# Sixteen operand products of a pair in one row, and six low-rank products kept together

## The chip, the cores and the metric

The kernel runs on one core of one Trainium2 chip. The metric is the device time of one execution in microseconds (us); the time before is the median of three runs, 1564.96 us (1563.26 to 1566.88). The profile is one execution recorded by the hardware profiler. Its engines are PE (TensorE, matrix products), PEld (its weight loads), DVE (VectorE), ACT (ScalarE), POOL (GpSimd) and SP (SyncE, which issues the transfers).

## The reference

Two layers of a hybrid decoder run over 512 tokens of width 1024 in float32. Each layer has one wide input projection, an RWKV-7 branch (8 heads of 64, a generalized delta rule), a latent attention branch, two gates, an output projection and a gated feed-forward with a convolution. What matters here is the RWKV-7 branch:

```python
log_w = -jax.nn.softplus(-(decay_base + jnp.tanh(p_w) @ w_decay_up)) - 0.5
decay = jnp.exp(-jnp.exp(log_w.astype(jnp.float32)))
iclr = jax.nn.sigmoid(iclr_base + p_a @ w_iclr_up)
kk = heads((p_k * k_k).astype(jnp.float32))
kk = kk * lax.rsqrt(jnp.sum(kk * kk, axis=-1, keepdims=True) + 1e-12)
k = p_k * (1.0 + (iclr - 1.0) * k_a)
...
def step(state, inp):
    r_t, w_t, k_t, v_t, a_t, b_t = inp
    sa = jnp.einsum('bhij,bhj->bhi', state, a_t)
    state = (state * w_t[:, :, None, :]
             + sa[..., None] * b_t[:, :, None, :]
             + v_t[..., None] * k_t[:, :, None, :])
    y_t = jnp.einsum('bhij,bhj->bhi', state, r_t)
    return state, y_t
```

The kernel does not step through 512 tokens. It cuts them into 8 chunks of 64, builds for each head and chunk the 128 x 128 product of scaled operands (`BK` with `AR`), masks it, solves the triangular part for all chunks, and then passes the state from chunk to chunk.

## The kernel before

Large products are done in three passes (high times high, low times high, high times low part of the operands; lines 253 to 255, tile `acc`). Weights come in units of eight 128 x 128 blocks, 24 products each; ACT rounds a unit to its high part (`whi`, line 203) and DVE takes the difference (`wlo`, line 204).

In the first stage of a layer the heads are taken in four pairs. The generator `pair(p)` is one pair's work in pieces, and a loop runs pieces of neighbouring pairs with projection and gate products between them. In order, `pair(p)` forms k, r and v; then two low-rank products `pw` and `pq` of 64 rows each, three passes (lines 540 and 541); from `pw` a Tanh on ACT (`z`, line 545), on DVE an addition (547) and a running sum (`L`, 550), from which come the decays; from `pq` another Tanh (`tad`, 560). Then come sums and transpositions for the normed key (570 and 578), the operands `AR` and `BK`, the bonus sum (618, read by 619) and v transposed (624, read by the copies to `Z` at 627). The last pieces are the operand products (635): for each half of the eight chunks, four chunks times two heads of the pair, into two banks `pA`. DVE multiplies both by the mask into `AM` (638), PE transposes `BKb` into a bank `pB` (643), and ACT copies that (644). The loop lets a gate's 24 products run between the halves. The low-rank products of pair p + 1 come just ahead of the operand products of pair p.

All these small results live in banks of one PSUM pool, tag `m`, with five buffers; three more hold `acc`. A bank can be written again when its last reader is done.

After the pairs comes the solve. DVE and ACT copy the triangular blocks (687), DVE transposes them (688) and works through 30 steps of a substitution (692, 694), transposes the result (696), and PE takes it from there (780). Meanwhile PE forms the latents (`lat`, read by DVE at 718).

The order on each engine is not the order of the code: a planner places every instruction by priorities and its own guess of when operands are ready. Within a `manual_schedule` block the named engine's instructions keep the order of the code. On the chip each engine then runs its list in that order; an instruction that waits holds up all behind it.

Of the kernel before, what the change touches and what calls it, by code (L numbers as in the profile page):

```python
# [159 lines left out]
def build(ctx, tc, x, pos, wst, vecd, constd, out):  # L160
    nc = tc.nc
    V, A, G, PE = nc.vector, nc.scalar, nc.gpsimd, nc.tensor
# [118 lines left out]
    def split(pool, src, scale, tag, bufs=None):  # L281

        hi = pool.tile([128, 512], F32R, name="hi", tag=tag, bufs=bufs)
        lo = pool.tile([128, 512], F32R, name="lo", tag=tag, bufs=bufs)
        if scale is None:
            A.copy(hi, src)
            V.tensor_tensor(lo, src, hi.bitcast(F32), ALU.subtract)
        else:
            A.activation(hi, src, AF.Copy, scale=scale)  # L289
            V.scalar_tensor_tensor(lo, src, scale, hi.bitcast(F32), ALU.mult, ALU.subtract)  # L290
        return hi, lo
# [141 lines left out]
    def mixer(l, ops, nrm, wks):  # L433
        with ExitStack() as mx:
            wk = wks.enter_context(pool(name=f"wk{l}", bufs=1))
            AM = wk.tile([128, 8, 8, 128], F32, name="AM")
            AR = [wk.tile([128, 8, 128], F32, name=f"AR{p}") for p in range(4)]
# [13 lines left out]
            with pool(name=f"ta{l}", bufs=2) as ta, pool(name=f"pa{l}", bufs=2, space=PSUM) as pa, \  # L451
# [7 lines left out]
                def mtile():  # L459
                    return pa.tile([128, 512], F32, name="m", tag="m", bufs=5)  # L460
# [62 lines left out]
                wah = split(ta, wa, None, "wah", 2)  # L523
                lw = []
# [5 lines left out]
                def pair(p):  # L530
# [4 lines left out]
                    v = shifted(4 + 3 * p, "v")  # L535
                    yield
                    pw, pq = mtile(), mtile()
                    for i, (w, xx) in enumerate(((0, 0), (0, 1), (1, 0))):
                        sl = slice(128 * p, 128 * p + 128)
                        PE.matmul(pw, lw[w][0:64, sl], wah[xx][0:64, :], start=i == 0, stop=i == 2)  # L540
                        PE.matmul(pq, lw[w][64:128, sl], wah[xx][64:128, :], start=i == 0, stop=i == 2)

                    z = TL("z")
                    z3 = z.rearrange("p (c t) -> p c t", t=65)
# [51 lines left out]
                    BK = ta.tile([128, 8, 128], F32, name="BK", tag="BK", bufs=2)  # L596
# [31 lines left out]
                               pV[64 * e:64 * e + 64, :].rearrange("p (c n) -> p c n", c=4))  # L628
                    yield

                    for hf in range(2):
                        pA = [mtile(), mtile()]
                        for c in range(4):
                            for hh in range(2):
                                PE.matmul(pA[hh][:, c * 128:c * 128 + 128], BK[64 * hh:64 * hh + 64, 4 * hf + c, :],  # L635
                                          AR[p][64 * hh:64 * hh + 64, 4 * hf + c, :], start=True, stop=True)
                        for hh in range(2):
                            V.tensor_tensor(AM[:, 2 * p + hh, 4 * hf:4 * hf + 4, :].rearrange("p (c e) n -> p c (e n)", e=2),
                                            pA[hh].rearrange("p (c n) -> p c n", c=2),
                                            maskA[:, None, :].to_broadcast([128, 2, 256]), ALU.mult)  # L640
                        pB = mtile()
                        for c in range(4):
                            PE.transpose(pB[:, c * 128:c * 128 + 128], BKb[:, 4 * hf + c, :], ident)  # L643
                        A.copy(BT[p][:, 4 * hf:4 * hf + 4, :].rearrange("p c n -> p (c n)"), pB)
                        yield

                pairs = [pair(p) for p in range(4)]
                for _ in range(3):
                    next(pairs[0])
# [30 lines left out]
            with pool(name=f"ti{l}", bufs=2) as ti, tc.manual_schedule(engines={PE.engine}):  # L680
# [95 lines left out]
                for b in range(2):  # L776
                    ps = sc()
                    for u in range(16 * b, 16 * b + 16):
                        for r0, c0 in half:
                            PE.matmul(ps[r0 + 32:r0 + 64, 32 * (u % 16):32 * (u % 16) + 32],  # L780
                                      AMu[r0:r0 + 32, u, c0 + 32:c0 + 64], T11[r0:r0 + 32, u, :],
                                      start=True, stop=True, tile_position=(r0, r0 + 32))
# [28 lines left out]
                for c in range(8):  # L811
                    i, e = divmod(c, 2)
# [17 lines left out]
                    for hd in (0, 4, 1, 5, 2, 6, 3, 7):  # L830
# [4 lines left out]
                                  start=True, stop=True, tile_position=(ur, ur))  # L835
# [173 lines left out]
    for l in range(DEPTH):  # L1009
# [7 lines left out]
        with pool(name=f"h{l + 1}", bufs=8, side="right") as hp, accs(f"accC{l}", 6):  # L1017
# [31 lines left out]
            with pool(name=f"ff{l}", bufs=44) as fp:  # L1049
# [11 lines left out]
                for i in range(FT):  # L1061
# [4 lines left out]
                    c = fp.tile([128, 528], F32, name="c", tag="ft", bufs=7)  # L1066
# [22 lines left out]
                if last:  # L1089
                    m = KT - 1  # L1090
                    ws = [W.get() for _ in range(FT)]
                    with tc.manual_schedule(engines={PE.engine}):
                        for f in range(2):
                            c = slice(256 * f, 256 * f + 256)
# [57 lines left out]
```

## Time and profile before

| | |
|---|---|
| median of the runs | 1564.96 us |
| the profiled execution, time | 1565.82 us |
| its span | 1564.0 us |
| mean granted clock of PE | 0.994 |
| PE busy | 1532.7 us, 98% |
| DVE busy | 913.5 us, 58% |
| ACT busy | 669.2 us, 43% |
| operand products (L635) | 256 instructions, 8 blocks of 16 in each layer |
| their place in the span | 83.8 to 182.5 us (layer 0), up to 955 us (layer 1) |

A row of the order of time has the start in us, the duration, the engine, the line, the operation, output and inputs, and the count of merged instructions; in brackets is the idle time of the engine ahead of it and what ended that. A float32 product counts as two instructions, so eight products are x16. A row of stretches has the start and end, the length, the busy time of PE with its instructions, the granted clock as a part of full speed, the share of the transfer engines and GB/s.

### The profile page before, as it was taken

The page shows a single profiled execution, that of the slowest core. Times are in us where ns is not written, and L with a number is a line of the kernel's source. Part 1 is how long each engine was busy: PE and PEld are TensorE (multiplying, and loading weights), DVE is VectorE, ACT ScalarE, POOL GpSimd, SP SyncE. Part 2 cuts the span into 40 slices and gives each one's busy share as a digit, 9 for nine tenths or more (in the row PEclk, how much of TensorE's full clock was granted, in tenths as well). Part 3 has the DMA queues.
Part 4 walks back from the last instruction along what each step waited for, and adds up shares of the span by engine and source line. Part 5 has one row for each costly group of instructions (what it writes and reads, how often), then busy time and mean ns, then how long its engine had stood idle before and what let it go on. Part 6 is the DMA issues. An engine that isn't in the chain of part 4 may idle for free.

```text
span 1564.0 us, 22128 instructions
## 1 busy us (share of the span) xinstructions
PE 1532.7 (98%) x8860; PEld 1233.0 (79%) x8860; DVE 913.5 (58%) x1510; ACT 669.2 (43%) x1020; POOL 184.4 (12%) x157
## 2 busy tenths in 40 slices
PE   8999999999999999999999999998999999999998
PEld 6888886668888888888878888765788888888887
DVE  6579795766555555533346768867564555554332
ACT  6445444663443333322244544457444333333222
POOL 1011101300311110100001121013012111100000
PEclk9999999999999999999999999999999999999999
DMA  6324322324323222333342333222352232222322
GB/s 208 115 95 139 124 83 69 96 86 155 122 89 101 95 95 94 100 116 115 108 149 94 109 108 117 81 65 92 101 171 92 96 106 95 94 95 96 103 98 81
DMA packets 57270, 166.05 MB, mean 106 GB/s; under 512 B 6352, under 2 KB 8528, under 8 KB 57168
## 3 DMA queue, kind: packets, MB, share of 16 engines
q1 hardware_dynamic: 57024, 164.48, 31.9%
q8 instruction: 69, 1.13, 0.3%
q14 instruction: 33, 0.27, 0.1%
q10 hardware_dynamic: 144, 0.16, 0.0%
HBM read 147.32 MB, written 17.30 MB: 105 GB/s over the span
## 4 chain that ended last, share of the span: by engine, by line
PE 92%; DVE 5%; ACT 1%; issue 1%; POOL 0%; DMA 0%; DVEq 0%; POOLq 0%; SPq 0%; ACTq 0%
PE acc L253 27%; PE acc L254 27%; PE acc L255 27%; PE sc L973 2%; PE pt L984 1%; PE po L992 1%; PE m L635 1%; DVE wlo L204 1%; PE xy L834 1%; PE m L643 1%; PE xy L844 1%; PE acc L947 1%; PE m L540 0%; DVE X L694 0%; DVE tm L692 0%
## 5 line engine op out<-in xcount | busy, mean ns | idle before, releaser
L253 PE MATMUL acc<-hi,whi 128*128 128x512 f32 (+1 forms) x1918 | 755.0, 394 | 6.1 <-ACT hi L289 5.2
L255 PE MATMUL acc<-hi,wlo 128*128 128x512 f32 (+1 forms) x1918 | 747.4, 390 | 0.8 <-DVE wlo L204 0.8
L254 PE MATMUL acc<-lo,whi 128*128 128x512 f32 (+1 forms) x1918 | 746.8, 389 | 0.0
L203 ACT CAST whi<-raw 128x1024 fp32r<-128x1024 f32 (+2 forms) x249 | 253.4, 1019 | 535.8 <-PE acc L254 463.3
L253 PEld LDWEIGHTS acc<-hi,whi 128*128 128x128 f32 x1918 | 361.2, 188 | 81.4 <-ACT hi L289 5.2
L255 PEld LDWEIGHTS acc<-hi,wlo 128*128 128x128 f32 x1918 | 361.2, 188 | 75.4 <-DVE wlo L204 1.3
L254 PEld LDWEIGHTS acc<-lo,whi 128*128 128x128 f32 x1918 | 361.5, 188 | 71.1 <-DVE lo L290 0.5
L204 DVE TENSOR_TENSOR wlo<-raw,whi 128x1024 fp32r<-128x1024 f32 (+2 forms) x249 | 303.3, 1220 | 178.2 <-ACT whi L203 177.8
L1072 POOL TENSOR_TENSOR c<-c,rstd 128x512 f32<-128x512 f32 x44 | 57.9, 1317 | 403.6 <-ACT c L1071 403.6
L1065 DVE TENSOR_TENSOR u<-acc,rstd 128x512 f32<-128x512 f32 x44 | 30.4, 692 | 104.4 <-PE acc L255 104.3
L1074 DVE TENSOR_TENSOR c<-c,acc 128x512 f32<-128x512 f32 x44 | 30.2, 687 | 86.4 <-POOL c L1072 86.4
L1071 ACT ACTIVATE c<-c 128x512 f32<-128x512 f32 x44 | 27.8, 632 | 81.7 <-DVE c L1070 81.7
L312 POOL TENSOR_TENSOR nv<-nv,cst 128x4 f32<-128x4 f32 (+1 forms) x10 | 10.0, 996 | 335.4 <-DVE nv L311 335.4
L348 POOL TENSOR_TENSOR nacc<-nacc,nsq 128x512 f32<-128x512 f32 x14 | 25.1, 1790 | 193.0 <-ACT nsq L347 193.0
L973 PE MATMUL sc<-K,q 128*128 128x128 f32 (+3 forms) x128 | 45.4, 451 | 1.3 <-DVE mn L976 1.0
L466 DVE TENSOR_TENSOR cur<-acc,rstd 128x512 f32<-128x512 f32 x28 | 19.1, 689 | 45.1 <-PE acc L255 37.6
L981 ACT ACTIVATE P<-P,mn 128x128 f32<-128x128 f32 (+3 forms) x64 | 35.1, 559 | 5.1 <-DVE mn L980 4.8
L979 ACT ACTIVATE P<-P,mn 128x128 f32<-128x128 f32 (+3 forms) x64 | 35.5, 556 | 3.7 <-DVE mn L976 3.5
L1068 ACT ACTIVATE c<-u,vec 128x512 f32<-128x512 f32 x44 | 35.7, 811 | 2.8 <-DVE u L1064 2.8
L976 DVE CUSTOM_DVE_ANT_0 P<-sc,cst 128x128 f32<-128x128 f32 (+3 forms) x64 | 30.4, 482 | 8.1 <-PE sc L973 5.5
L1070 DVE SCALAR_TENSOR_TENSOR c<-u,vec,c 128x512 f32<-128x512 f32 x44 | 33.1, 752 | 1.5
L1069 DVE SCALAR_TENSOR_TENSOR c<-u,vec,c 128x512 f32<-128x512 f32 x44 | 32.8, 746 | 1.8 <-ACT c L1068 1.8
(243 smaller groups left out, 1318.5 us busy)
## 6 DMA issues: line engine op xcount, KB each, us to landing
raw<-in_w SPq DMA_DIRECT2D x238, 512.0 KB, 3.3
gate_d<-gg SPq DMA_DIRECT2D x32, 256.0 KB, 2.0
AM<-gate_d SPq DMA_DIRECT2D x16, 256.0 KB, 4.2
gb<-gate_d SPq DMA_DIRECT2D x16, 256.0 KB, 3.2
h<-in_x SPq DMA_DIRECT2D x8, 256.0 KB, 4.3
rgate_d<-gt SPq DMA_DIRECT2D x8, 256.0 KB, 2.5
bl_d<-rk SPq DMA_DIRECT2D x8, 256.0 KB, 4.2
bl<-bl_d SPq DMA_DIRECT2D x8, 256.0 KB, 2.6
```

Source lines behind the costliest of these rows:

```text
L203: A.copy(hi, r)
L204: V.tensor_tensor(lo, r, hi.bitcast(F32), ALU.subtract)
L253: PE.matmul(ps, w[0], xx[0], start=first, stop=False)
L254: PE.matmul(ps, w[0], xx[1], start=False, stop=False)
L255: PE.matmul(ps, w[1], xx[0], start=False, stop=last)
L973: PE.matmul(sp[:, 0:n], qs[hh][:, 128 * b:128 * b + 128], ks[hh][:, 0:n], start=True, stop=True)
L979: A.activation(P[:, 0:n], P[:, 0:n], AF.Exp, bias=mn[:, 0:1], scale=-1.0, accum_out=mn[:, 1:2])
L981: A.activation(P[:, 0:n], P[:, 0:n], AF.Copy, scale=mn[:, 2:3])
L1068: A.activation(cc, u[:, 2:514], AF.Identity, bias=vc(l, "conv_b", i), scale=vc(l, "conv_w", 2 * FT + i))
L1069: V.scalar_tensor_tensor(cc, u[:, 1:513], vc(l, "conv_w", FT + i), cc, ALU.mult, ALU.add)
L1070: V.scalar_tensor_tensor(cc, u[:, 0:512], vc(l, "conv_w", i), cc, ALU.mult, ALU.add)
L1072: G.tensor_tensor(cc, cc, rstd, ALU.mult)
```

## The change

```diff
@@ pair(p)
                     pw, pq = mtile(), mtile()
-                    for i, (w, xx) in enumerate(((0, 0), (0, 1), (1, 0))):
-                        sl = slice(128 * p, 128 * p + 128)
-                        PE.matmul(pw, lw[w][0:64, sl], wah[xx][0:64, :], start=i == 0, stop=i == 2)
-                        PE.matmul(pq, lw[w][64:128, sl], wah[xx][64:128, :], start=i == 0, stop=i == 2)
+                    with tc.manual_schedule(engines={PE.engine}):
+                        for i, (w, xx) in enumerate(((0, 0), (0, 1), (1, 0))):
+                            sl = slice(128 * p, 128 * p + 128)
+                            PE.matmul(pw, lw[w][0:64, sl], wah[xx][0:64, :], start=i == 0, stop=i == 2)
+                            PE.matmul(pq, lw[w][64:128, sl], wah[xx][64:128, :], start=i == 0, stop=i == 2)
...
+                    pAs = [[mtile(), mtile()] for _ in range(2)]
+                    with tc.manual_schedule(engines={PE.engine}):
+                        for c in range(8):
+                            for hh in range(2):
+                                PE.matmul(pAs[c // 4][hh][:, c % 4 * 128:c % 4 * 128 + 128], BK[64 * hh:64 * hh + 64, c, :],
+                                          AR[p][64 * hh:64 * hh + 64, c, :], start=True, stop=True)
                     for hf in range(2):
-                        pA = [mtile(), mtile()]
-                        for c in range(4):
-                            for hh in range(2):
-                                PE.matmul(pA[hh][:, c * 128:c * 128 + 128], BK[64 * hh:64 * hh + 64, 4 * hf + c, :],
-                                          AR[p][64 * hh:64 * hh + 64, 4 * hf + c, :], start=True, stop=True)
+                        pA = pAs[hf]
                         for hh in range(2):
```

The same products are computed from the same operands. All sixteen products of a pair now stand in one row and write four banks, which are taken together; masks, transposes and copies stay in the two halves. The six low-rank products of a pair can no longer have another product between them. In the changed program the lines of the pair are named one higher up to the products (540 and 541 are 541 and 542), and three higher behind them (638 is 641, 643 is 646, 687 is 690, 718 is 721); the products are 636.

**PE, the first pair of layer 0**, from the last low-rank products of pair 1 to the first gate product. `m` is a bank, `AR_203` and `BK` the operands, `BKb` what is transposed; in brackets the engines whose progress an instruction waits for. Before:

```order
L540 MATMUL m<-hi,lw_429 128x512
L541 MATMUL m<-hi,lw_429 128x512
L635 MATMUL m<-AR_203,BK 128x128 [waits DVE_49,PE_49]
L635 MATMUL m<-AR_203,BK 128x128 [waits PE_49,Activation_49]
L635 MATMUL m<-AR_203,BK 128x128 x6
L643 MATMUL m<-cst,BKb 128x128 [waits DVE_49,Pool_49]
L643 MATMUL m<-cst,BKb 128x128 x3
L253 MATMUL acc<-hi,whi 128x512
```

and now:

```order
L541 MATMUL m<-hi,lw_429 128x512
L542 MATMUL m<-hi,lw_429 128x512
L636 MATMUL m<-AR_203,BK 128x128 [waits DVE_49,PE_49]
L636 MATMUL m<-AR_203,BK 128x128 [waits PE_49,Activation_49]
L636 MATMUL m<-AR_203,BK 128x128 x6
L636 MATMUL m<-AR_203,BK 128x128 [waits DVE_49]
L636 MATMUL m<-AR_203,BK 128x128 [waits Activation_49]
L636 MATMUL m<-AR_203,BK 128x128 x6
L646 MATMUL m<-cst,BKb 128x128 [waits DVE_49,Pool_49]
L646 MATMUL m<-cst,BKb 128x128 x3
L253 MATMUL acc<-hi,whi 128x512
```

The second eight products moved up by 24 gate products, with their waits on DVE and ACT; the transposes of the first half now stand behind all sixteen. In pairs 1 and 2, and in layer 1, the same moved.

**DVE, the same place**: the rows from the gate's product to the masks, as they stand now.

```order
L478 TENSOR_TENSOR gg<-acc,rstd 128x512
L204 TENSOR_TENSOR wlo<-raw,whi 128x1024
L548 TENSOR_SCALAR z<-z 128x8x64
L551 SCALAR_TENSOR_TENSOR L<-d_222,z 128x520
L641 TENSOR_TENSOR AM<-m,cst 128x512 x2
L611 TENSOR_TENSOR AR_204<-r,z 128x4x2x64
L641 TENSOR_TENSOR AM<-m,cst 128x512 x2
```

Down to the first two masks and L611 these rows are those of before, one for one; the second two masks came some rows later and follow at once now.

**DVE, where the solve begins** in layer 0, behind the last pair's masks. Before:

```order
L478 TENSOR_TENSOR gg<-acc,rstd 128x512
L204 TENSOR_TENSOR wlo<-raw,whi 128x1024
L638 TENSOR_TENSOR AM<-m,cst 128x512 x2
L687 COPY DX<-AM 32x1024 x2
L688 STREAM_TRANSPOSE X<-DX 128x1024
L692 TENSOR_TENSOR tm<-X 128x30
L694 TENSOR_TENSOR X<-X,tm 128x30
L692 TENSOR_TENSOR tm<-X 128x58
L718 TENSOR_TENSOR lat_1828<-acc,rstd 128x512
```

and now:

```order
L641 TENSOR_TENSOR AM<-m,cst 128x512 x4
L478 TENSOR_TENSOR gg<-acc,rstd 128x512
L204 TENSOR_TENSOR wlo<-raw,whi 128x1024
L690 COPY DX<-AM 32x1024 x2
L721 TENSOR_TENSOR lat_1852<-acc,rstd 128x512
L691 STREAM_TRANSPOSE X<-DX 128x1024
L204 TENSOR_TENSOR wlo<-raw,whi 128x1024
L695 TENSOR_TENSOR tm<-X 128x30
```

The last masks moved ahead of the gate's product, and the first latent's product moved ahead of the transposition that opens the solve. It is the same in layer 1. On SP only transfers of the rotary tables and of pair 2's bonus changed places with their neighbours, in layer 0.

## The prediction

> **What bounds the kernel now.** I read the page's span and chain of waits first, then the list of who waited for whom, then the order of time on PE, DVE and ACT around one product block.
>
> ```profile
> span 1564.0 us, 22128 instructions
> ...
> PE 1532.7 (98%) x8860; PEld 1233.0 (79%) x8860; DVE 913.5 (58%) x1510; ACT 669.2 (43%) x1020; POOL 184.4 (12%) x157
> ...
> PE 92%; DVE 5%; ACT 1%; issue 1%; POOL 0%; DMA 0%; DVEq 0%; POOLq 0%; SPq 0%; ACTq 0%
> ```
>
> TensorE carries the chain. Whatever makes PE stand still or saves it an instruction slot is paid or earned in full; work on DVE and ACT counts only where PE is made to wait for it. So the question is which waits the new order puts in front of PE. This is one block of products, pair 0 of layer 0, in order of time on PE:
>
> ```profile
> 83.04 0.50 PE L540 MATMUL m<-hi,lw 64*128 64x512 f32 x1
> ...
> 83.84 1.06 PE L635 MATMUL m<-AR,BK 64*128 64x128 f32 x16
> 84.84 0.66 PE L643 MATMUL m<-cst,BKb 128*128 128x128 f32 x4
> 85.25 0.47 PE L253 MATMUL acc<-hi,whi 128*128 128x512 f32 x1
> ...
> 90.59 0.39 PE L255 MATMUL acc<-hi,wlo 128*128 128x512 f32 x1
> 90.91 1.16 PE L635 MATMUL m<-AR,BK 64*128 64x128 f32 x16
> 92.00 0.66 PE L643 MATMUL m<-cst,BKb 128*128 128x128 f32 x4
> 92.41 0.48 PE L253 MATMUL acc<-hi,whi 128*128 128x512 f32 x1
> 92.72 0.40 PE L254 MATMUL acc<-lo,whi 128*128 128x512 f32 x1
> ```
>
> PE never stops here: low-rank products of the next pair from 83.04, eight products in 1.00 us, four transposes in 0.41, then 24 gate products (85.25 to 90.59 are 23 steps, 0.23 each), then the other eight products and four transposes. The readers are far behind. On ACT and on DVE, the same stretch:
>
> ```profile
> 85.41 0.69 ACT L545 ACTIVATE z<-m,der 128x512 f32<-128x512 f32 x1
> ```
>
> ```profile
> 84.04 0.68 DVE L478 TENSOR_TENSOR gg<-acc,rstd 128x512 f32<-128x512 f32 x1
> 84.64 1.21 DVE L204 TENSOR_TENSOR wlo<-raw,whi 128x1024 fp32r<-128x1024 f32 x1
> 86.13 0.43 DVE L547 TENSOR_SCALAR z<-z 128x512 f32<-128x512 f32 x1 [0.28 <-ACT z L545]
> 86.66 1.24 DVE L550 TENSOR_TENSOR_SCAN L<-d,z 128x520 f32<-128x520 f32 x1
> 87.82 1.26 DVE L638 TENSOR_TENSOR AM<-m,cst 128x512 f32<-128x512 f32 x2
> ```
>
> The Tanh that reads `pw` ends at 86.10, 2.3 us behind the start of the products. The mask that reads the first product bank ends at about 88.50 (two take 1.26, one 0.68), 3.7 us after the products. Today this lag costs nothing, because the 5.4 us of gate products lie between the block and the next request for those banks.
>
> **The change part by part.** *Banks.* There are five `m` banks. At the block of pairs 0, 1 and 2 they hold: one free, `pV` (read by the copies to Z), the bonus sum (read by L619), `pw` (read by the Tanh L545), `pq` (read later still). Now the first half takes the free one and that of `pV`, the transposes that of the sum; the second half comes 24 products later and takes `pw`'s bank and the first product bank again. After the change four banks are wanted at once: the fourth is `pw`'s, so the second product of the second half waits for the Tanh; and the transposes behind the sixteen products then find only the bank of the first products, so they wait for the first mask. These are the two waits that stand in the order shown above; the built program's wait counts are those of this Tanh and this mask. PE works in order, so behind them stand the 24 gate products and everything else.
>
> *Price of a block.* Nothing ahead of the Tanh or the first mask moves on ACT or DVE, and none of it waits for the held instructions, so both end when they end now. How soon PE follows a release is in the solve's rows further down: a transposition ends at 222.73 + 2.18 = 224.91 and PE starts at 224.97, 0.06 later. So the transposes start at 88.56. Without waits they would start at 83.84 + 2 x 1.00 = 85.84. PE loses 2.72 us, in two gaps: about 85.0 to 86.16 and 87.15 to 88.56. The first gap adds nothing by itself, since the mask ends last. The shortest case is pair 2 in layer 1, here on PE and on DVE:
>
> ```profile
> 924.99 0.66 PE L643 MATMUL m<-cst,BKb 128*128 128x128 f32 x4
> ```
>
> ```profile
> 927.73 1.26 DVE L638 TENSOR_TENSOR AM<-m,cst 128x512 f32<-128x512 f32 x2
> ```
>
> There the loss is (927.73 + 0.66 + 0.06) - (924.99 + 1.00) = 2.46. I take 2.72 for pairs 0 and 1 and 2.46 for pair 2 in both layers: 4 x 2.72 + 2 x 2.46 = **15.8 us**. Pair 3 pays nothing: no low-rank products of a next pair hold banks then, and its fourth bank was read long before. Bounds: nothing, if the waits were met early, to 6 x 3.7 = 22 if the whole lag of the mask came into PE's way.
>
> *What merging saves.* The second block today costs 92.72 - 90.59 = 2.13 us from the last gate product to the second one behind it. Of that remain eight products behind their own kind, 1.00, and four transposes among full-array products. For those the nearest row is another set of four:
>
> ```profile
> 75.79 0.39 PE L255 MATMUL acc<-hi,wlo 128*128 128x512 f32 x1
> ...
> 76.69 0.40 PE L254 MATMUL acc<-lo,whi 128*128 128x512 f32 x1
> ```
>
> that is 0.90 over the same places. Saved: 0.23 a pair, 1.8 for eight. The fixed six low-rank products change the order only in pair 2 of layer 0, where the bonus product L618 stood between them:
>
> ```profile
> 150.81 0.50 PE L540 MATMUL m<-hi,lw 64*128 64x512 f32 x1
> ...
> 152.24 1.05 PE L635 MATMUL m<-AR,BK 64*128 64x128 f32 x16
> ```
>
> 1.43 us against 0.80 (83.04 to 83.84) plus a slot of 0.23 for L618: 0.4 saved. Together **-2.2 us**; this is the whole gain that the edit can have.
>
> *The solve.* The masks of pair 3's second half come earlier, but DVE's queue now has the first latent's product (L718) ahead of the transposition L688. In both layers DVE is then busy without a break worth naming up to L696, for which PE waits. On PE and on DVE:
>
> ```profile
> 182.53 0.66 PE L643 MATMUL m<-cst,BKb 128*128 128x128 f32 x4
> ...
> 224.97 1.20 PE L780 MATMUL sc<-T,AM 32*32 32x32 f32 x64 [0.35 <-DVE T L696]
> ```
>
> ```profile
> 187.03 2.11 DVE L688 STREAM_TRANSPOSE X<-DX 128x1024 f32<-128x1024 f32 x1 [0.75 <-ACT DX L687]
> ...
> 222.73 2.18 DVE L696 STREAM_TRANSPOSE T<-X 128x1024 f32<-128x1024 f32 x1
> ```
>
> The latent needs 24 products behind the transposes at 182.53, so it is summed at 182.53 + 0.41 + 5.34 + 0.39 = 188.7, and L688 starts 0.6 later, at 189.3 instead of 187.03. From the 2.24 go the 0.6 of L718, which no longer lies inside the chain, and some 0.4 of short idle times in it: L696 ends 1.3 later against PE, whose wait grows from 0.35 to 1.6. Twice: **+2.5 us** (0 to 4.5).
>
> *The clock.* The profile of before shows what follows when PE stands idle in short pieces. Stretches of 3.41 us, busy time and granted clock of PE:
>
> ```profile
> 248.79:252.20 3.41, 1.79 (x50) 1.00 0.73 240
> 252.20:255.61 3.41, 3.41 (x24) 0.51 0.38 145
> 1061.15:1064.57 3.42, 1.43 (x7) 1.00 0.03 8
> 1064.57:1067.98 3.41, 3.41 (x11) 0.51 0.00 0
> 1081.63:1085.05 3.42, 2.42 (x11) 1.00 0.22 77
> ```
>
> A stretch with 1.79 or 1.43 us of work is followed by one at half clock; one with 2.42 is not. A new block has 2.6 us of idle time within 3.6. If the stretches are cut at fixed times, a stretch with at least 1.62 us idle (3.41 - 1.79) falls into the block for half of all positions; were 0.99 enough (3.41 - 2.42), for all. I take three in four, 4.5 of six blocks, at 3.41 x 0.5 = 1.7 us each: **+7.6 us** (0 to 10.2).
>
> The Trainium skill, "TensorE: Matmul & The Clock Gate", Part 1 and "Why this matters for your kernels", says that the clock falls after an idle window of about 3.4 us and asks for no idle gap over about 3 us between bursts. Read so, gaps of 1.2 and 1.4 us would leave the clock alone and the sum would be 7.6 lower; the rows at 248.79, where no gap is that long, speak against this reading.
>
> *Sum.* 15.8 - 2.2 + 2.5 + 7.6 = +23.7 us. The profiled execution took 1565.82 for a span of 1564.0, 0.9 over the median of 1564.96. So its span would be 1587.7 and the median 1564.96 + 23.7 = **1588.7 us**.
>
> **The rivals.** *The clock stays full.* If only a whole stretch without work halves it, the sum is +16.1: **1581**. For it: the new gaps hold about 1 us of products between them. Against it: the stretch at 248.79 held 1.79 us in three pieces and still was followed by half clock. This is also what the page's sentence gives.
>
> *Neither wait holds PE: faster.* If Tanh and mask were done when PE asks, only the merge remains: -2.2, **1563**. That needs the mask to end by 85.84 instead of 88.50, 2.7 us sooner. DVE would have to put it ahead of L204, L547 and L550, whose 1.21, 0.43 and 1.24 make up the lag. The new queue has them ahead of it still.
>
> *The change does nothing measurable.* The stalls would have to be taken back from waits that PE has today. All of PE's idle time is 31 us (1564.0 less 1532.7 busy), spread over places that wait for PE's own results and move along with it. I see nothing to repay 16.
>
> **How the numbers follow.** Likeliest, with 0.75: both waits in six blocks, the clock halved behind several; own range 1582 to 1593 (two to six halved stretches, solve 0 to 4.5). Clock full 0.15 (1578 to 1583). Faster 0.06. Nothing measurable 0.04. The likeliest gives the time, 1588.7. The range reaches down over the clock-full case to 1575, and up to 1598, where the stalls come nearer their upper bound. About 0.2%, 3 us, is what a measurement of this kernel can tell from no change: faster 0.06, same 0.04, slower 0.90.
>
> **What would show it.** In the changed profile: PE idle twice in each of six blocks, ahead of the products for the Tanh (about 1.1 us) and ahead of the transposes for the mask (about 1.4); pair 3 without either; 0.90 around the transposes that now stand alone; L696 waited for by about 1.6 us; stretches of half clock just behind the blocks. It is wrong if the blocks run through in 2.0 us, or if the mask ends much earlier than 3.7 us behind its products. If the stalls are there and the clock is full, only the last term failed.

## The result and the profile after

The changed kernel takes 1590.72 us (median of five runs, 1589.37 to 1592.63) against 1566.88 us for the kernel before on the same chip (five runs, 1563.26 to 1567.98): a ratio of 1.0158, with a 95% interval of 1.0147 to 1.0169. It is 23.8 us slower; the prediction said 23.7.

The page of the changed kernel, its span, the first row of busy times and the chain of waits:

```profile
span 1590.8 us, 22135 instructions
...
PE 1541.1 (97%) x8860; PEld 1241.9 (78%) x8860; DVE 914.5 (57%) x1510; ACT 669.5 (42%) x1020; POOL 184.1 (12%) x157
...
PE 87%; DVE 8%; ACT 2%; issue 2%; POOL 1%; DMA 0%; SPq 0%; DVEq 0%; POOLq 0%
```

PE runs the same 8860 instructions. Its idle time rose from 31.3 (1564.0 - 1532.7) to 49.7 us (1590.8 - 1541.1), and its busy time by 8.4 us with no more work. Idle time is a wait; more busy time for the same work points to a slower clock, which the stretches below show. DVE and ACT, which had 6% of the chain, now have 10%.

The list of who waited for whom, the three rows of PE that the change made or lengthened most (in all, times, longest):

```profile
PE m L646 <- DVE AM L641: 7.9, 6, 1.3
...
PE m L636 <- ACT z L546: 5.6, 6, 1.1
...
PE sc L783 <- DVE T L699: 4.3, 2, 2.2
```

Six waits for the mask, six for the Tanh, two for the solve; only the last stood in the profile before, at 0.7. Together they are 17.1 of the 18.4 us of new idle time (17.8 less 0.7). Among the other rows the wait for POOL's `Z` grew from 4.0 to 5.2. In order of time on PE, pair 0, then pair 3 of layer 0:

```profile
86.10 1.29 PE L636 MATMUL m<-AR,BK 64*128 64x128 f32 x18
88.39 1.16 PE L636 MATMUL m<-AR,BK 64*128 64x128 f32 x14 [1.00 <-ACT z L546]
90.87 1.09 PE L646 MATMUL m<-cst,BKb 128*128 128x128 f32 x4 [1.32 <-DVE AM L641]
...
186.52 2.06 PE L636 MATMUL m<-AR,BK 64*128 64x128 f32 x32
188.50 0.66 PE L646 MATMUL m<-cst,BKb 128*128 128x128 f32 x4
```

The nine products up to the first that lacks a bank run (x18), PE stands for the Tanh, runs seven more, and stands for the mask. Pair 3 runs its sixteen through in 1.98 us. What PE stood for, on DVE:

```profile
90.06 1.26 DVE L641 TENSOR_TENSOR AM<-m,cst 128x512 f32<-128x512 f32 x2
```

Two masks take 1.26, so the first ends near 90.7, and the transposes follow at 90.87. PE's stretches of 3.413 us, laid so that the changes of the granted clock fall on their edges:

```profile
87.41:90.82 3.41, 1.16 (x14) 1.00 0.93 318
90.82:94.24 3.42, 3.37 (x10) 0.50 0.28 114
162.50:165.92 3.42, 2.24 (x32) 1.00 0.82 264
165.92:169.33 3.41, 2.65 (x14) 1.00 0.51 197
872.48:875.89 3.41, 2.09 (x19) 1.00 0.83 323
944.16:947.57 3.41, 1.81 (x24) 1.00 0.88 302
947.57:950.98 3.41, 2.90 (x9) 0.50 0.27 101
```

Behind the stretch that holds pair 0's waits (1.16 us of work) and the one of pair 2 in layer 1 (1.81) a stretch runs at half clock. The waits of pair 2 in layer 0 fall into two stretches (2.24 and 2.65), and behind neither, nor behind pair 0 in layer 1 (2.09), does one. With the other two, which hold 1.39 and 1.67 us of work and are followed by half clock, four of the six blocks pay the clock.

Laying both profiles' landmarks side by side (start of a block's products to that of the next one's): the six blocks cost 4.10, 3.71 and 2.14 us more in layer 0 and 2.55, 3.89 and 3.61 in layer 1, 20.0 in all; the stretch from pair 3's products to the solve's first product costs 1.51 and 1.47 more. That is 23.0 of the 26.8 us between the two spans. The other 3.8 are mainly halved stretches elsewhere: one at 22.5 us, ahead of anything that the change touches (2.2), and more of them in layer 1's solve. The profiled execution of after lies 1.9 us above its median and that of before 1.1 below; this is what separates 26.8 from 23.8.

### The profile page after: what moved, and what is told of

The parts are those of the page before. It is cut to its first block, busy times and chain, and to the rows that moved or that the text cites. A ratio compares the mean times of both kernels' runs of the same rounds, so it can differ in the third digit from the quotient of the medians.

```text
span 1590.8 us, 22135 instructions
## 1 busy us (share of the span) xinstructions
PE 1541.1 (97%) x8860; PEld 1241.9 (78%) x8860; DVE 914.5 (57%) x1510; ACT 669.5 (42%) x1020; POOL 184.1 (12%) x157
## 4 chain that ended last, share of the span: by engine, by line
PE 87%; DVE 8%; ACT 2%; issue 2%; POOL 1%; DMA 0%; SPq 0%; DVEq 0%; POOLq 0%
PE acc L253 26%; PE acc L255 25%; PE acc L254 25%; PE sc L976 2%; PE pt L987 1%; PE po L995 1%; DVE wlo L204 1%; DVE X L697 1%; DVE tm L695 1%; PE m L646 1%; PE xy L837 1%; PE xy L847 1%; POOL mu L905 1%; DVE L L551 0%; DVE gg L478 0%
## 5 line engine op out<-in xcount | busy, mean ns | idle before, releaser
L478 DVE TENSOR_TENSOR gg<-acc,rstd 128x512 f32<-128x512 f32 x20 | 13.7, 686 | 39.3 <-PE acc L255 39.3
L1073 DVE SCALAR_TENSOR_TENSOR c<-u,vec,c 128x512 f32<-128x512 f32 x44 | 33.1, 752 | 1.5
```

What stands on the lines that cost most here:

```text
L1073: V.scalar_tensor_tensor(cc, u[:, 0:512], vc(l, "conv_w", i), cc, ALU.mult, ALU.add)
```

## The experiments

**Is it the banks?** The theory of the prediction: the row of sixteen needs four `m` banks at once, of which one is still read by the Tanh, and the transposes find only the bank that the mask still reads. If so, each wait must vanish with one bank lent from elsewhere, and the computation stays as it is. The first run takes the transposes' bank `pB` from the accumulator pool, the second also the fourth product bank.

```diff
-                        pB = mtile()
+                        pB = acc() if p < 3 and hf == 0 else mtile()
```

> The changed kernel, but in pairs 0 to 2 the transposes behind the sixteen products write an acc bank and no longer want the first product bank. Bank theory: the six waits for the mask go, the six for the Tanh (5.6 us in the changed kernel) stay, no half clock behind the blocks since one gap of 1.1 us leaves a stretch at least 2.3 us of work; solve as dear as before (+3.6). 1566.9 + 7.0 - 1.8 + 3.6 = 1575.7 (1573 to 1579). Rival, sixteen products in a row cost by themselves or by the clock alone: 1590.7 as the changed kernel. Rival, the clock stays full whatever the gaps: only the 7.9 us of mask waits go, 1582.8.

Measured: 1579.89 us (1578.63 to 1580.59), ratio 1.0085 (1.0070 to 1.0101).

```diff
-                    pAs = [[mtile(), mtile()] for _ in range(2)]
+                    pAs = [[mtile(), mtile()], [mtile(), acc() if p < 3 else mtile()]]
...
-                        pB = mtile()
+                        pB = acc() if p < 3 and hf == 0 else mtile()
```

> As the run with one acc bank, and the fourth product bank too is an acc bank in pairs 0 to 2, so that no instruction of the block waits for the Tanh or the mask. Bank theory: both waits gone in all six blocks, sixteen products in 2.0 us, the merge's saving of 1.8 is kept, solve +3.6: 1566.9 - 1.8 + 3.6 = 1568.7 (1566 to 1572). Rival, the row itself is what costs: 1590.7. Rival, the loan of two acc banks makes the gates wait instead: PE waits ahead of L253 behind the blocks, 1575 or more.

Measured: 1572.94 us (1569.28 to 1574.56), ratio 1.0037 (1.0023 to 1.0051). PE's waits with one bank lent:

```profile
PE m L636 <- ACT z L546: 5.6, 6, 1.1
...
PE sc L783 <- DVE T L699: 4.3, 2, 2.2
```

and with both:

```profile
PE sc L783 <- DVE T L699: 4.3, 2, 2.2
...
PE acc L253 <- DVE gg L478: 0.9, 2, 0.4
```

With one bank the six waits for the mask are gone and the six for the Tanh stay, at the same length. With both, no wait is left at a block; the lent banks cost 0.9 us where an accumulator comes late. So the banks are the cause of the waits in the blocks: 10.8 us of the 23.8 go with the first one, 7.0 with the second. Both runs stand some 4 us above what was expected. Their profiles have seven and six halved stretches where before has four (without the one behind PE's last product), most of them at the solve, and at 1.7 us each these are 5.1 and 3.4 us that the expectations did not have.

**Which pairs pay?** The merged row for pairs 0 to 2 alone (pair 3 as in the kernel before), and for pair 3 alone.

```diff
+                    one = p < 3
+                    if one:
+                        pAs = [[mtile(), mtile()] for _ in range(2)]
...
                     for hf in range(2):
-                        pA = pAs[hf]
+                        if one:
+                            pA = pAs[hf]
+                        else:
+                            pA = [mtile(), mtile()]
+                            for c in range(4):
...
```

> The changed kernel, but pair 3 of each layer has its products in two halves as before. Bank theory: the six stalls stay (13.5 us of waits), the solve's order is the one of before, so PE waits 0.35 for the transposed inverse instead of 2.1: 1590.7 - 3.6 + 0.5 = 1587.6, or down to 1584 if a halved stretch at the solve goes with it. Rival, each merged pair costs a quarter: 1566.9 + 0.75 x 23.8 = 1584.8 with the long wait at the solve still there.

> Only pair 3 of each layer has its sixteen products in a row, pairs 0 to 2 as before. Bank theory: no wait inside any block, but DVE takes the first latent ahead of the solve: PE waits about 2.1 instead of 0.35 for L696 in each layer. 1566.9 + 3.6 - 0.5 = 1570 (1568.5 to 1574 with a halved stretch or two behind that wait). Rival, each merged pair costs a quarter of 23.8: 1572.9, with waits in the block of pair 3. Rival, the solve's order does not matter: 1566.4.

Measured: 1586.32 us (1583.84 to 1586.89) for pairs 0 to 2, and 1571.5 (1569.83 to 1575.49) for pair 3 (`p == 3` in place of `p < 3`). PE's waits with pairs 0 to 2 merged:

```profile
PE m L655 <- DVE AM L650: 8.0, 6, 1.3
...
PE m L638 <- ACT z L546: 5.6, 6, 1.1
...
PE sc L792 <- DVE T L708: 0.7, 2, 0.4
```

and with pair 3 merged:

```profile
PE sc L792 <- DVE T L708: 4.3, 2, 2.2
```

The two parts split cleanly by their waits. Pairs 0 to 2 have all twelve block waits and cost 19.4 us over the 1566.9 of before; pair 3 has the solve wait alone and costs 4.6. Together that is 24.0, against 23.8 measured for the change; the spread of the medians would hide a difference of a us or two.

**Does the clock follow the gaps?** The changed kernel with 50 added products of 0.23 us that nobody reads (into a spare accumulator bank), placed where PE stood: four (two in pair 2) ahead of the second eight products and five ahead of the transposes. The waits are thereby covered, not removed: the Tanh and the mask end when they end. The computation is the same; 50 x 0.23 = 11.5 us of work is added to it.

```diff
+                        def keep(n):
+                            for _ in range(n if p < 3 else 0):
+                                PE.matmul(junk, blkr, wah[0], start=True, stop=True)
                         for c in range(8):
+                            if c == 4:
+                                keep(4 if p < 2 else 2)
...
+                        keep(5)
```

> The changed kernel with work added that nobody reads: in each block of pairs 0 to 2 products of 128x512 into a spare acc bank, 4 (pair 2: 2) ahead of the product that waits for the Tanh, 5 ahead of the transposes that wait for the mask, 50 in all, 0.23 us each. Clock theory (a stretch of 3.41 us with less than about 1.8 us of work halves the next): the added 11.4 us run inside the gaps, block lengths stay, the halved stretches behind the blocks vanish: 1590.7 - 6 = 1584.5 (1582 to 1587), faster with more work. Rival, the gaps cost by their length alone: 1590.7 unchanged. Rival, the gaps are no free room: 1602.

Measured: 1587.47 us (1585.85 to 1588.15), ratio 1.0123 (1.0109 to 1.0138). The first block, in order of time on PE:

```profile
84.04 1.06 PE L644 MATMUL m<-AR,BK 64*128 64x128 f32 x16
85.04 1.20 PE L638 MATMUL acc<-hi,blkr 128*128 128x512 f32 x4
86.17 1.32 PE L644 MATMUL m<-AR,BK 64*128 64x128 f32 x16
87.42 1.43 PE L638 MATMUL acc<-hi,blkr 128*128 128x512 f32 x5
88.82 0.63 PE L655 MATMUL m<-cst,BKb 128*128 128x128 f32 x4
```

The transposes start 4.78 us after the first product (88.82 - 84.04), as in the changed kernel (90.87 - 86.10 = 4.77): PE is as late as before, but busy. No block is followed by half clock now, and the kernel with more work is 3.2 us faster. So the clock really is a term of its own and is paid for the gaps. The gain is smaller than was expected, and the time lies just above the range given. In the two profiled executions ten halved stretches became six, 4 x 1.7 = 6.8 us, and the spans differ by 4.5 (1590.8 - 1586.3). Outside the blocks six are halved in each. From start to start the six blocks cost 14.3 us more than before, where the changed kernel's 20.0 are 13.2 without its four halved stretches: the added products are not quite free, by some 1.2 us. The rest lies outside the blocks.

**What makes the solve late?** The prediction named the first latent's product, which now stands ahead of the transposition that opens the solve. To undo that in the changed kernel, it is held behind the first half of the substitution's second step, as before (the expectations call it the third step).

```diff
...
+                    if s == 2:
+                        after = op.ins
...
-                    V.tensor_tensor(o, ps, rstd, ALU.mult)
+                    with tc.issue_after(after):
+                        V.tensor_tensor(o, ps, rstd, ALU.mult)
```

> The changed kernel with one order fixed on DVE: the first latent's product comes only behind the third step of the substitution, as in the kernel before. Theory: L696 ends sooner, PE's wait for it falls from 2.1 to about 0.8 in each layer: 1590.7 - 2.6 = 1588.1 (1585 to 1589 with halved stretches at the solve gone). Rival, DVE's total is what counts and its order not: 1590.7, wait unchanged.

Measured: 1592.08 us (1590.67 to 1593.1), ratio 1.0153 (1.0139 to 1.0168): no gain. The same edit with both banks lent:

> Both repairs: two acc banks lent to the block in pairs 0 to 2, and the first latent behind the third step of the substitution. Theory: what is left is the merge's saving of 1.8 against some 0.9 of longer wait at the solve: 1566.9 - 0.9 = 1566.0 (1563.5 to 1568), no measurable difference from before. Rival, something else of the change still costs: 1570 or more.

Measured: 1571.28 us (1569.21 to 1575.83), against 1572.94 (1569.28 to 1574.56) without it, which is no difference that these ranges show, and with the same wait at the solve. DVE's rows show why, here with the banks as in the change. In the changed kernel:

```profile
200.59 0.69 DVE L721 TENSOR_TENSOR lat<-acc,rstd 128x512 f32<-128x512 f32 x1 [2.40 <-PE acc L255]
201.20 2.09 DVE L691 STREAM_TRANSPOSE X<-DX 128x1024 f32<-128x1024 f32 x1
```

and with the first latent held:

```profile
197.15 2.09 DVE L691 STREAM_TRANSPOSE X<-DX 128x1024 f32<-128x1024 f32 x1 [0.50 <-ACT DX L690]
199.95 1.23 DVE L204 TENSOR_TENSOR wlo<-raw,whi 128x1024 fp32r<-128x1024 f32 x1 [0.71 <-ACT whi L203]
...
216.54 0.16 DVE L311 TENSOR_SCALAR nv<-sc 128x4 f32<-128x4 f32 x1 [1.88 <-PE sc L332]
```

The transposition does start earlier, but further down DVE's list stands an instruction on token sums that PE has not yet formed, at an earlier step of the substitution than in the kernel before. DVE stands 1.88 us there with the rest of the substitution behind it. So the next runs held these two instructions (behind steps 14 and 16, their places of before), with both banks lent; once with the first latent held and once without.

```diff
+                    stops.append(V.tensor_tensor(X[:, s + 1:32, 0:s], X[:, s + 1:32, 0:s], tm, ALU.add).ins)
...
+                    with tc.issue_after(stops[14 if i == 0 else 16]):
                         return rsqrt_tok(ssq, n, NORM_EPS, pool=ti, tag="lsq", bufs=3)
```

> The merged products with both lent banks and the first latent product held behind the second step of the substitution, and now also the two VectorE instructions on the token sums (L311) held where the kernel before has them: behind the 14th and the 16th step of the substitution. In the run without that, VectorE stood 4.6 us in four waits for the token sums of TensorE at L311, 2.3 us a layer, with the rest of the substitution behind them. Theory 1 (the substitution's end is set by the place of the token sums in VectorE's queue: an earlier start is stood off again at L311): T ends about 2 us sooner a layer, TensorE's wait for T falls from 2.15 to between 0.1 and 0.5 us a layer, the waits at L311 fall under 1 us in all, and the time is 1571.3 - 2 x 1.8 = 1567.7 us, 1565 to 1569.5 with one halved clock stretch more or less. Theory 2 (something behind the sums, the rotation or the weight splits, fixes the end): the wait for T stays near 2.15 us a layer and the time at 1571 us.

> The merged products with both lent banks; the token sums' VectorE instructions (L311) are held behind the 14th and the 16th step of the substitution, the first latent product stays ahead of the substitution. In the changed kernel VectorE stood 1.15 us a layer at L311. Theory 1: only those 1.15 us can be won, so TensorE's wait for T falls from 2.15 to about 1.0 us a layer and the time from 1572.9 to about 1570.6 us (1568.5 to 1572.5). Theory 2 (the end is fixed further on): the wait stays at 2.15 and the time at 1572.9 us.

Measured: 1572.72 us (1567.55 to 1577.0) and 1572.27 (1567.38 to 1577.33). PE's wait for T and DVE's row, with both held:

```profile
PE sc L788 <- DVE T L702: 3.9, 2, 2.0
```

```profile
209.63 0.69 DVE L725 TENSOR_TENSOR lat<-acc,rstd 128x512 f32<-128x512 f32 x1 [1.93 <-PE acc L255]
```

The waits at the token sums are gone (0.2 us in all), and DVE stands as long at the fourth latent's product. Holding that too, behind step 19, in the kernel with lent banks and in the changed kernel itself:

```diff
-                    with tc.issue_after(after):
+                    with tc.issue_after(after if i < 3 else stops[19]):
```

> The run with both lent banks and held sums, with the fourth latent product (L725) now also held where the kernel before has it, behind the 19th step of the substitution; it had stood behind the 17th, and VectorE waited 1.93 us there for TensorE. Theory 1 (VectorE's queue is in order, and each instruction that waits for TensorE pins what is behind it; the planner's places for four such instructions are the solve term): the last of the pins goes, four step instructions of 0.42 us move ahead of it, and TensorE's wait for T falls from 1.95 to 0.2 to 0.6 us a layer. The time falls by 2 x 1.6 = 3.2 us, and by more if the halved clock stretches around the solve leave with the wait: from 1572 to about 1567.5 us (1565 to 1570). Theory 2 (something else still fixes T): the wait stays near 1.9 us and the time near 1572 us.

> The changed kernel itself, without lent banks, with the same four instructions held: the first latent product behind the 2nd step, the token sums behind the 14th and the 16th, the fourth latent product behind the 19th. Theory 1: the block waits stay (7.9 us at the masks, 5.6 us at the Tanh), the wait for T falls from 2.15 to 0.2 to 0.6 us a layer, and the time from 1590.7 by 2 x 1.7 to about 1587.3 us (1585 to 1590). Theory 2: the wait for T stays near 2 us a layer and the time near 1591 us.

Measured: 1571.16 us (1569.53 to 1572.75) and 1590.48 (1589.55 to 1594.79). The wait for T and DVE's row, with lent banks:

```profile
PE sc L788 <- DVE T L702: 3.9, 2, 1.9
```

```profile
209.88 0.69 DVE L325 TENSOR_TENSOR rq<-sc,tab 128x512 f32<-128x512 f32 x1 [1.93 <-PE sc L319]
```

The planner had moved a fourth instruction that reads PE's result to the same place. In this whole row of runs the first theory failed, and the wait stayed where the second had it, at 1.9 to 2.15 us. What they show: the late T is not the place of one instruction. In the runs that hold the first latent, each further one that was held left DVE standing about 1.9 us at the next one that waits for PE, and PE's wait for T fell by no more than 0.3 us. Between its two transpositions DVE does the same work as in the kernel before, 35.3 us, but its stands there are 5.1 us in the last run with lent banks against 2.5. Besides the 1.93 there is one more that none of these runs held. The first weight split, which before came behind the second step, now stands ahead of the first:

```profile
190.01 1.22 DVE L204 TENSOR_TENSOR wlo<-raw,whi 128x1024 fp32r<-128x1024 f32 x1 [1.34 <-ACT whi L203]
```

What stays open is whether DVE's whole list of before, weight splits included, kept under the merged pair 3, would bring the wait back to 0.35; no run has it.

**The merge without its costs.** Pairs 0 to 2 merged with both banks lent, pair 3 as in the kernel before:

> The sixteen products in a row for pairs 0 to 2 alone, with both of their banks lent from the accumulators; pair 3 as in the kernel before. If the block waits are the missing banks and the solve wait is pair 3's, neither is left: time of before 1566.9 less six merges of 0.23 us, plus up to 0.9 us of waiting for a lent bank = 1566.4 us (1564.5 to 1568), no wait at the masks, 0.4 us a layer or less at the solve. If the costs of the parts simply add: both banks lent 1572.9 less 4.6 of pair 3 alone = 1568.3 us.

Measured: 1565.57 us (1562.27 to 1568.16, twelve runs), before 1567.0; ratio 0.9991, interval 0.9981 to 1.0001. Its span and its wait at the solve:

```profile
span 1565.5 us, 22127 instructions
...
PE sc L792 <- DVE T L708: 0.7, 2, 0.4
```

No block wait, no long solve wait, and a time that can't be told from that of the kernel before. The estimate from the rows was 1566.4, half a microsecond below before; the times can neither show nor exclude a gain of that size. The profiles show it in the blocks. Pair 0 of layer 1, the start of its products and that of the next pair's, before and then in this run (a row ends where another bank is written):

```profile
856.48 1.06 PE L635 MATMUL m<-AR,BK 64*128 64x128 f32 x16
...
890.21 1.05 PE L635 MATMUL m<-AR,BK 64*128 64x128 f32 x16
```

```profile
858.85 1.06 PE L638 MATMUL m<-AR,BK 64*128 64x128 f32 x16
...
892.25 1.16 PE L638 MATMUL m<-AR,BK 64*128 64x128 f32 x17
```

That is 33.73 us before and 33.40 now. Five of the six blocks are 0.29 to 0.38 us shorter; the sixth, pair 1 of layer 0, is 0.04 longer. In all that is 1.6 us. In the run with pair 3 alone merged, which leaves these pairs as before, the same six lengths differ from those of before by at most 0.04. The rest of the span was 3.0 us longer in this execution; 1.4 of it is one more wait for POOL's `Z` (5.4 us in all against 4.0), which other runs of this series have or lack without the merge deciding it.

Whether the costs of the parts simply add can't be told from the times. By medians both banks lent less pair 3's 4.6 would be 1568.3; by ratios it would be 1.0037 - 0.0035 = 1.0002, with an interval of about 0.0014 to either side of each.

**What the six low-rank products do.** The section on the change said that they can no longer have another product between them, and the prediction gave 0.4 us to that. The built programs contradict it. With that lock alone, every engine's list is row for row that of the kernel before, and with the sixteen in a row alone it is row for row that of the changed kernel. In the list of the lock alone the bonus product still stands between them:

```
L541 MATMUL m<-hi,lw_427 128x512
L542 MATMUL m<-hi,lw_427 128x512
L619 MATMUL m<-lo,blkr 128x512
L541 MATMUL m<-lo,lw_427 128x512
L542 MATMUL m<-lo,lw_427 128x512
```

The lock fixes the order of its own instructions among each other and does not keep others out. Everything measured here belongs to the sixteen in a row; the bonus product moved because the planner placed things anew.

## Why the prediction was right, point by point

- *Banks.* Right in each part: the waits are those of Tanh and mask, they go one by one with one bank each, and pair 3 has none.
- *Price of a block.* 2.72 us was worked out for pairs 0 and 1. In pair 0 the transposes start 4.77 us behind the first product, where 2.00 would do: 2.77. For pair 2, 166.68 - 162.31 - 2.00 = 2.37 was measured in layer 0 and 2.54 in layer 1, against 2.46. All six give 16.1 us against 15.8. The rows for pair 2 in layer 0:

```profile
162.31 1.27 PE L636 MATMUL m<-AR,BK 64*128 64x128 f32 x18
...
166.68 0.63 PE L646 MATMUL m<-cst,BKb 128*128 128x128 f32 x4 [1.32 <-DVE AM L641]
```

  The two waits of pair 0 add to 2.3, the loss is 2.8: in two pieces its sixteen products take 1.29 + 1.16 = 2.45 us to the end of the last, where the estimate counts 2.00 from start to start. The term was right because it was worked from start to start and not from the idle times. The first gap alone adds nothing while the mask ends last, as said; once the mask's bank was lent, the same gaps for the Tanh became what is paid, 7.0 us.
- *What merging saves.* Small, as said, and near in size: with both banks lent five of six blocks are some 0.3 us shorter where 0.23 was taken. The 0.4 us ascribed to the fixed low-rank products came too (161.49 to 162.31 in pair 2 of layer 0, 0.82 us against 1.43 with the bonus product between them), but from the planner's new places. In the time of the whole kernel nothing of this can be told (0.9991, 0.9981 to 1.0001).
- *The solve.* The step that was mis-sized, with a cause that did not hold. Said were 1.6 us a layer and +2.5 in all; measured are 2.15 and 2.12, and +3.6. The late first latent is there as described (DVE stands 2.40 us for it), but undoing it won nothing, since DVE then stands elsewhere. I looked at one instruction that moved and should have compared every DVE instruction in the stretch that waits for another engine.
- *The clock.* Right in kind and near in number: 4.5 halved blocks were taken, four came, at 1.7 us each, 6.8 for 7.6. In the three other profiles that have both waits (pairs 0 to 2 merged, and the two runs on the solve without lent banks) three or four came. The stretches are cut at fixed times: the halved ones begin at 90.82 and 947.57, 251 lengths of 3.4133 us apart, and the others of this profile fall on the same grid. So the position of a block in this grid decides, as the guess of three in four assumed.
- *Clock stays full* (1581) fell with the halved rows. The Trainium skill, "TensorE: Matmul & The Clock Gate", Part 1, says that the window is about 3.4 us and runs freely; the fixed grid agrees, 3.413 us. It also says that the half clock comes after at least one idle window. The trace does not agree: the stretch ahead of 90.82 held 1.16 us of work and that ahead of 947.57 held 1.81, and no gap in either block exceeds 1.4 us.
- *Neither wait holds* would have needed the mask 2.7 us sooner; it ended as late behind its products as before. *Nothing measurable* would have needed other waits to repay the stalls; PE's other large waits stayed or grew, for `hi` (L289) from 5.2 to 5.7 us and for POOL's `Z` from 4.0 to 5.2.

The forecast of 1588.7 lies 2.0 us under the median. Most of this is that before's own median on the day was 1566.88 and not the 1564.96 that the sum started from; the difference, 23.7, is off by 0.1. That is better than its terms are, and luck. For the six blocks the terms give 15.8 + 7.6 - 6 x 0.23 - 0.4 = 21.6, and 20.0 was measured; for pair 3 and the solve 2.5 - 2 x 0.23 = 2.0, and 3.0 was measured. The halved stretches that have nothing to do with the blocks differ from one execution to the next.

## What to carry to other kernels

Before two groups of products are merged into one row, count the banks that the row and what follows it ask for at once, and look for the reader that frees each: here two missing banks of five turned a lag of 3.7 us that cost nothing into 18 us. Waits on a nearly full PE should be priced with the stretch of half clock that can follow them: here two waits of up to 1.1 and 1.3 us close together were followed by it in three or four of six blocks; the first alone, with one bank lent, in none. A way to see that price is to fill the gaps with products nobody reads. Where a planner places the instructions, an edit in one place gives another order in the next stage too, and holding single instructions here only moved the stand to the next one that waits.

## What the runs showed of the hardware

- A stretch need not be idle to be followed by half clock. In the blocks of the changed kernel stretches with 1.16 to 1.81 us of work of 3.41 were, and stretches with 2.09 or more were not. Elsewhere the boundary is not clean: one with 2.06 us of large products was followed by half clock at 22.56, one of the solve with 2.32 us, nearly all of it 32 x 32 products, at 241.01, and one with 1.73 us was not. The three rows:

```profile
19.14:22.56 3.42, 2.06 (x13) 1.00 0.27 73
...
237.60:241.01 3.41, 2.32 (x129) 1.00 0.03 5
...
1087.52:1090.93 3.41, 1.73 (x10) 1.00 0.03 9
```

- Not even idle time is needed. In the run with one bank lent a stretch that the profile shows as full, most of it small products (32 instructions of 64 x 64 and 16 with a single column), was followed by half clock:

```profile
202.54:205.96 3.42, 3.42 (x52) 1.00 0.16 61
205.96:209.37 3.41, 3.41 (x10) 0.50 0.45 154
```

  That small products count for less than their busy time would fit this row and the one at 241.01; no run tests it.
- Half clock can stay for several stretches. With both banks lent, one stretch of 1.26 us of work at the solve was followed by four halved ones, which lose 6.8 us, all of them full of work (many small products):

```profile
224.41:227.82 3.41, 1.26 (x54) 1.00 0.00 0
227.82:231.23 3.41, 3.41 (x91) 0.50 0.02 5
...
238.06:241.47 3.41, 3.41 (x22) 0.50 0.02 5
```

  In the kernel before the same small products run at full clock, where no long wait precedes them:

```profile
224.98:228.39 3.41, 3.41 (x134) 1.00 0.02 5
```

  Why the clock comes back after one stretch behind a block of pairs and after up to four here was not tested; that the small products hold it down is only a reading of these rows. Halved stretches are part of why the run with both banks lent lies 6 us above before: its profile has two more of them, 3.4 us, beside 3.6 us of longer waits at the solve.
- The same program spreads by these stretches. Twelve executions with both banks lent and the sums held took 1567.55 to 1577.0 us, and the mean granted clock went from 0.995 to 0.989 with them: 0.006 x 1570 = 9.4 us, which is about the whole spread.
